# The second MLP's first products begun inside the output products, and low weight parts made by an adding DMA

## The chip, the cores and the metric

The kernel runs on one core of one Trainium2 chip. Its time is the device time of one execution in microseconds (us); of several executions the median counts. The core has a matrix engine (TensorE, PE in the profile), a vector engine (VectorE, DVE), a scalar engine (ScalarE, ACT), GpSimd (POOL) and SyncE (SP), which here only issues DMAs. Each runs its own queue in order; between them there are semaphores.

## The reference

Two layers work on 512 latent tokens and 256 context tokens of 1024 features in fp32. Layer 0 mixes tokens with gated linear attention, layer 1 with 2-D neighbourhood attention of 16 heads; each is followed by a gated MLP with a convolution of width 3 over tokens. What the change touches is the end of layer 1:

```python
x_lat = x_lat + g1_l * o_l                     # o_l: heads @ w_out of the attention
h_l = modulate(x_lat, norm2_g[i], sh2_l, s2_l) # rms_norm(x, g) * (1 + scale) + shift

def conv_ffn(h, w_in, conv_w, conv_b, w_out):
    a, val = jnp.split(h @ w_in, 2, axis=-1)   # 1024 -> 2 x 2816
    ap = jnp.pad(a, ((0, 0), (1, 1), (0, 0)))
    a = ap[:, :-2] * conv_w[0] + ap[:, 1:-1] * conv_w[1] + ap[:, 2:] * conv_w[2] + conv_b
    return (jax.nn.silu(a) * val) @ w_out
```

The result is `x_lat + g2_l * conv_ffn(h_l, ...)`, normalized once more. In layer 1 only the latent tokens go through this MLP.

## The kernel before

**Products in three parts.** Every fp32 operand is held as a rounded high part and a low part that is the rest. `mm3` (L287 to L290) issues three products for one: low weight by high data (L288), high weight by low data (L289), high by high (L290), all into one PSUM group. Names ending in `h` are high parts, in `l` low parts: `wh`, `wl` weights; `hh`, `hl` the normalized tokens `H`; `oh`, `ol` the attention's heads; `uh`, `ul` the MLP's inner values.

**Weights.** `wunit` (L269) brings 128 x 1024 fp32 of weights, 512 KB, by a DMA on SP's queue into one of three buffers `st`. ACT writes the rounded copy `wh` (L283), DVE subtracts, `wl` = `st` - `wh` (L284). Both go into a slot of a ring of five slots of 1024 columns, which the weights take in the order of the program; a slot is free when the last product with its old weights is done.

**Output products of the attention.** `out_group(m, d, a, b)` multiplies two units of `w_no` by the heads of two pairs for one block d of 128 features and tokens a to b, six products into a PSUM bank of the pool `ps_mm` (three banks; the other five banks are `ps_aux`). DVE adds the result, gated, to the residual `xl` (L312). The last two pairs (m = 3) are done in two halves of 256 tokens, eight blocks each.

**Norm.** `Norm` follows block by block. `add` squares a block on ACT (L333, L336) and adds it to `nacc` on DVE (L337). `stats` multiplies `nacc` by ones (TensorE, L344), scales (DVE `ms`, L346), takes the power -1/2 (POOL `rs`, L348) and spreads it over the partitions (TensorE, L351). `apply` makes one block of `H`: `hf` on DVE (L371), `hh` on ACT (L372), `hl` on DVE (L373). The first half's `stats` and `apply` calls stand between the output blocks of the second half; the second half's come after the last block.

**The MLP, `ffn1`.** 2816 inner features are 22 tiles of 128, in six groups of three and one of four. A tile takes two units of `w_fi`, for `a` and `val`; each has 8 x 3 products. `a` goes by ACT into a padded row `apad` (L1079), through the convolution on DVE (L808, L811, L812) and silu on ACT (L813), times `val` (`u`, L1103), split into `uh` (L300) and `ul` (L301). Then the group's units of `w_fo` give output products for eight blocks d. The first group's tiles 0 and 1 are done by `in_first`: their four units of weights, then for the first token half all four product groups (tile, unit), then for the second half all four, each group running its eight blocks k before the next starts. The other tiles run over 512 tokens at once.

**Order.** A scheduler orders each engine's instructions, so that program order is kept only as far as its own estimates do; a table for silu is loaded on ACT once ahead of the first silu. Weights are asked for as slots and buffers come free.

## Time and profile before

| | us |
|---|---|
| median of 3 runs | 1702.51 (1701.19 to 1707.1) |
| the profiled execution | 1703.84 |
| its span | 1702.1 |
| TensorE busy | 1643.6 (97%) |
| DVE busy | 1190.5 (70%) |
| ACT busy | 740.5 (44%) |
| POOL busy | 217.4 (13%) |

In the profiled execution the output products in token halves begin at 1303.03 us of the span, the norm's second half is spread at 1328.60, tiles 0 and 1 end and tile 2 begins at 1347.37, and the first group's output products start at 1358.28. A later group of three tiles begins at 1375.08 and its output products at 1407.74.

To read the rows: a timeline row has start, duration, engine, line, operation, what is written and read, the count, and in brackets the idle time ahead of it with the engine and line that ended it. Starts of pipelined matmuls lie closer than their durations.

### The profile page before, as it was taken

The page shows a single profiled execution, that of the slowest core. Times are in us where ns is not written, and L with a number is a line of the kernel's source. Part 1 is how long each engine was busy: PE and PEld are TensorE (multiplying, and loading weights), DVE is VectorE, ACT ScalarE, POOL GpSimd, SP SyncE. Part 2 cuts the span into 40 slices and gives each one's busy share as a digit, 9 for nine tenths or more (in the row PEclk, how much of TensorE's full clock was granted, in tenths as well). Part 3 has the DMA queues.
Part 4 walks back from the last instruction along what each step waited for, and adds up shares of the span by engine and source line. Part 5 has one row for each costly group of instructions (what it writes and reads, how often), then busy time and mean ns, then how long its engine had stood idle before and what let it go on. Part 6 is the DMA issues. An engine that isn't in the chain of part 4 may idle for free.

```text
span 1702.1 us, 27128 instructions
## 1 busy us (share of the span) xinstructions
PE 1643.6 (97%) x10867; PEld 1409.3 (83%) x10867; DVE 1190.5 (70%) x1973; ACT 740.5 (44%) x1331; POOL 217.4 (13%) x321
## 2 busy tenths in 40 slices
PE   6999999999999999999999999999999999999997
PEld 3768777777899999999999778888887888888887
DVE  4797877785998886878767675666667755555555
ACT  3665746563753432433425454334344522222232
POOL 1021212220000000000000043433332000000000
PEclk9999999999999999999999999999999999999999
DMA  6653513113323332424223042334331233232321
GB/s 257 190 176 108 175 61 107 33 51 137 100 87 124 124 112 68 149 84 159 79 84 102 10 132 92 109 117 130 99 114 61 87 100 95 94 95 75 111 87 50
DMA packets 54190, 179.70 MB, mean 106 GB/s; under 512 B 7024, under 2 KB 10864, under 8 KB 54064
## 3 DMA queue, kind: packets, MB, share of 16 engines
q1 hardware_dynamic: 54064, 177.97, 32.4%
q8 instruction: 85, 1.39, 0.3%
q14 instruction: 41, 0.34, 0.1%
HBM read 173.75 MB, written 2.10 MB: 103 GB/s over the span
## 4 chain that ended last, share of the span: by engine, by line
PE 79%; DVE 10%; ACT 5%; issue 2%; DMA 2%; POOL 2%; SPq 0%; POOLq 0%; ACTq 0%; DVEq 0%
PE mm L288 16%; PE mm L290 15%; PE mm L289 15%; PE aux L288 8%; PE aux L289 8%; PE aux L290 8%; PE mm L1252 2%; PE aux L1235 2%; PE aux L1210 2%; DMA st<-in 1%; DVE t L571 1%; PE aux L650 1%; PE aux L615 1%; ACT wh L283 1%; DVE t L570 1%
## 5 line engine op out<-in xcount | busy, mean ns | idle before, releaser
L288 PE MATMUL mm<-hh,wl 128*128 128x512 f32 (+3 forms) x864 | 306.8, 357 | 5.3 <-ACT hh L372 2.5
L289 PE MATMUL mm<-hl,wh 128*128 128x512 f32 (+3 forms) x864 | 301.4, 350 | 0.4 <-DVE hl L301 0.4
L290 PE MATMUL mm<-hh,wh 128*128 128x512 f32 (+3 forms) x864 | 301.5, 350 | 0.0
L289 PE MATMUL mm<-ul,wh 128*128 128x512 f32 (+1 forms) x544 | 188.3, 347 | 0.2 <-DVE ul L301 0.2
L288 PE MATMUL mm<-uh,wl 128*128 128x512 f32 (+1 forms) x544 | 188.4, 348 | 0.0
L290 PE MATMUL mm<-uh,wh 128*128 128x512 f32 (+1 forms) x544 | 188.4, 347 | 0.0
L288 PEld LDWEIGHTS mm<-hh,wl 128*128 128x128 f32 (+1 forms) x864 | 162.6, 189 | 29.7 <-issue 5.1
L283 ACT ACTIVATE wh<-st 128x1024 fp32r<-128x1024 f32 (+1 forms) x127 | 131.8, 1051 | 121.5 <-issue 69.4
L312 DVE SCALAR_TENSOR_TENSOR xl<-mm,mod,xl 128x512 f32<-128x512 f32 (+1 forms) x168 | 116.1, 697 | 96.2 <-PE mm L290 95.8
L289 PEld LDWEIGHTS mm<-hl,wh 128*128 128x128 f32 (+1 forms) x864 | 163.1, 189 | 18.6 <-issue 0.8
L290 PEld LDWEIGHTS mm<-hh,wh 128*128 128x128 f32 (+1 forms) x864 | 162.9, 189 | 18.6 <-issue 0.8
L284 DVE TENSOR_TENSOR wl<-st,wh 128x1024 fp32r<-128x1024 f32 (+1 forms) x126 | 155.1, 1237 | 30.6 <-ACT wh L283 30.1
L288 PE MATMUL aux<-hh,wl 128*128 128x384 f32 (+2 forms) x496 | 173.8, 351 | 0.0
L289 PE MATMUL aux<-hl,wh 128*128 128x384 f32 (+2 forms) x496 | 173.7, 350 | 0.0
L290 PE MATMUL aux<-hh,wh 128*128 128x384 f32 (+2 forms) x496 | 173.4, 350 | 0.0
L263 ACT ACTIVATE wh<-st 128x512 fp32r<-128x512 f32 (+1 forms) x126 | 94.1, 756 | 164.7 <-issue 57.0
L348 POOL TENSOR_TENSOR rs<-ms,mhalf 128x2 f32<-128x2 f32 (+1 forms) x10 | 10.0, 1004 | 931.5 <-DVE ms L346 931.5
L288 PEld LDWEIGHTS mm<-uh,wl 128*128 128x128 f32 x544 | 102.2, 188 | 15.7 <-ACT uh L300 2.0
L289 PEld LDWEIGHTS mm<-ul,wh 128*128 128x128 f32 x544 | 102.4, 188 | 14.8 <-DVE ul L301 0.4
L264 DVE TENSOR_TENSOR wl<-st,wh 128x512 fp32r<-128x512 f32 (+1 forms) x126 | 104.6, 847 | 12.7 <-ACT wh L263 12.1
L290 PEld LDWEIGHTS mm<-uh,wh 128*128 128x128 f32 x544 | 102.3, 188 | 13.2
L288 PEld LDWEIGHTS aux<-hh,wl 128*128 128x128 f32 x496 | 93.5, 189 | 8.8 <-issue 1.4
(324 smaller groups left out, 3254.7 us busy)
## 6 DMA issues: line engine op xcount, KB each, us to landing
st<-in SPq DMA_DIRECT2D x201, 512.0 KB, 3.7
sa<-in SPq DMA_DIRECT2D x98, 512.0 KB, 3.8
sx<-in SPq DMA_DIRECT2D x14, 512.0 KB, 7.0
xl<-in SPq DMA_DIRECT2D x8, 512.0 KB, 5.5
xc<-in SPq DMA_DIRECT2D x4, 512.0 KB, 7.5
out<-y SPq DMA_DIRECT2D x16, 128.0 KB, 1.7
raw<-in SPq DMA_DIRECT2D x16, 96.0 KB, 2.5
t<-q SPq DMA_DIRECT2D x16, 64.0 KB, 2.1
```

Of the source, the lines that this page charges most:

```text
L263: nc.scalar.activation(hi, s_, AF.Copy)
L264: nc.vector.tensor_sub(lo, s_, hi.bitcast(F32))
L283: nc.scalar.activation(hi, st, AF.Copy)
L284: (eng or nc.vector).tensor_sub(lo, st, hi.bitcast(F32))
L288: mm(out, a[1], b[0], start=first, stop=False, **at)
L289: mm(out, a[0], b[1], start=False, stop=False, **at)
L290: mm(out, a[0], b[0], start=False, stop=last, **at)
L312: nc.vector.scalar_tensor_tensor(x_, ps, gate(l, n, d, rng), x_, OP.mult, OP.add)
L570: nc.vector.tensor_mul(eq, eq, st[h]["q"])
L1210: mm(pss[hh][:, off:off + 256], qe[a_][p_, 128 * t:128 * t + 128], ke[b_][p_, ks], start=i == 0, stop=i == 2)
L1235: nc.tensor.transpose(pT[:, i * 128:(i + 1) * 128], S2[:, o:o + 128], ident)
L1252: mm(po[64 * hh:64 * hh + 64, 128 * t:128 * t + 128], V[:, vs[i], 64 * hh:64 * hh + 64], PTs[hh][:, i * 128:(i + 1) * 128], start=i == 0, ...
```

## The change

**Low parts.** `wunit(..., added=True)` makes the low part without DVE: ACT writes the high part, and also writes `st` times -1 into the low slot, in the same rounded type, so that it holds minus the high part; then a DMA on POOL's queue, with add as its accumulating operation, brings the same weights from HBM once more and adds them there; the sum is rounded into the low slot. The weights in HBM are read twice. This is done for all 44 units of `w_fi` and 22 of `w_fo` of layer 1 and for the last two units of `w_no`: 68 more DMAs of 512 KB, 68 fewer subtractions. `st` is freed by ACT.

**Order of the products.** The two last units of `w_no` and the first of the MLP are asked for in the last head pair, the next two among the first half of the output products. `Begun` holds the weights and banks of tiles 0 and 1. Within the second half of the output products, from block 3 on, and around the second norm's statistics, the first token half is multiplied for three groups at once, (tile 0, a), (tile 0, val), (tile 1, a), block by block (`first3`), in two banks of `ps_aux`, two groups sharing a bank. `stats` is cut into `rms` and `spread_rms`. The weights of the fourth group, (tile 1, val), are asked for behind the second norm's power on POOL (`issue_after` lets what is inside it be placed only behind the given instruction); its first-half products come after the spread. The second token half is then done for all four groups at once, block by block, each behind the `apply` that makes its block, in two banks of `ps_mm`. `in_first` only copies `apad` and finishes. The ring's slots of these four units are, in the order of use, those that the second unit of tile 2 and the first three units of `w_fo` take next.

The places where this moves instructions, in each engine's order. First POOL, from the end of the attention to the end of the program, before (`rs` is the power; buffer numbers stand behind names) and after:

```order
L1225 TENSOR_SCALAR S_12787<-S_12787,ri 128x512 x2
L348 TENSOR_TENSOR rs_13017<-ms_13015,mhalf 128x2
L348 TENSOR_TENSOR rs_13137<-ms_13135,mhalf 128x2
L1067 MEMSET apad_13178 128x1 x2
L1067 MEMSET apad_13179 128x1 x2
L348 TENSOR_TENSOR rs_15597<-ms_15595,mhalf 128x2
L348 TENSOR_TENSOR rs_15753<-ms_15751,mhalf 128x2
```

```order
L1261 TENSOR_SCALAR S_12802<-S_12802,ri 128x512 x2
L286 DMA wl<-in 128x1024 x2
L356 TENSOR_TENSOR rs_13034<-ms_13032,mhalf 128x2
L356 TENSOR_TENSOR rs_13210<-ms_13208,mhalf 128x2
L286 DMA wl<-in 128x1024 x2
L1104 MEMSET apad_13396 128x1 x2
L1104 MEMSET apad_13397 128x1 x2
L286 DMA wl<-in 128x1024 x61
L356 TENSOR_TENSOR rs_15661<-ms_15659,mhalf 128x2
L356 TENSOR_TENSOR rs_15817<-ms_15815,mhalf 128x2
```

After, five of the low parts' DMAs stand ahead of the first power, two of them in this piece; the first of the two right behind the second norm's power, `rs_13210`, is the fourth group's.

Next TensorE, around the second norm's spread (the row with `ident`), one piece of before and two of after; products of `hh` and `hl` are the MLP's:

```order
L290 MATMUL mm<-hh,wh 128x256
L344 MATMUL aux<-ones,nacc 128x2 x2
L288 MATMUL mm<-hh,wl 128x256 x2
L289 MATMUL mm<-hl,wh 128x256
L290 MATMUL mm<-hh,wh 128x256
L351 MATMUL aux<-ident,rs_13137 128x128 x2
L288 MATMUL mm<-hh,wl 128x256
L288 MATMUL aux<-hh,wl 128x256
L289 MATMUL aux<-hl,wh 128x256
```

```order
L293 MATMUL aux<-hl,wh 128x256
L294 MATMUL aux<-hh,wh 128x256
L352 MATMUL aux<-ones,nacc 128x2 x2
L364 MATMUL aux<-ident,rs_13210 128x128
L292 MATMUL aux<-hh,wl 128x256 x2
L364 MATMUL aux<-ident,rs_13210 128x128
L293 MATMUL aux<-hl,wh 128x256
L294 MATMUL aux<-hh,wh 128x256
```

```order
L294 MATMUL mm<-hh,wh 128x256
L292 MATMUL mm<-hh,wl 128x256
L293 MATMUL mm<-hl,wh 128x256
L294 MATMUL mm<-hh,wh 128x256
L292 MATMUL mm<-hh,wl 128x256
L292 MATMUL aux<-hh,wl 128x256
L293 MATMUL aux<-hl,wh 128x256
L294 MATMUL aux<-hh,wh 128x256
L292 MATMUL aux<-hh,wl 128x256
```

The first piece is before, the second after at the same place, the third after some 17 rows later. Before, the last first-half products of the two `a` groups stand between ones and spread, and the first-half products of (tile 0, val), the `aux` rows, behind it. After, the spread's first row stands right behind the ones, and blocks 6 and 7 of the three groups behind it. The third piece shows the end of seven second-half products (into `mm`) and the first products of the fourth group (into `aux`), which read the low part that POOL's DMA makes.

Last ACT, at the end of tiles 0 and 1, before and after (`apad` copies close the tiles' `a`, `wl` and `wh` fill slots, `tt` is silu):

```order
L1079 ACTIVATE apad_13178<-mm 128x256
L1079 ACTIVATE apad_13179<-mm 128x256
L1079 ACTIVATE apad_13178<-mm 128x256
L283 ACTIVATE wh<-st 128x1024 x2
L813 ACT_TABLE_LOAD
L813 ACTIVATE tt<-tt 128x512
L1079 ACTIVATE apad_13179<-mm 128x256
L283 ACTIVATE wh<-st 128x1024
L300 ACTIVATE uh<-u 128x512
L283 ACTIVATE wh<-st 128x1024
L813 ACTIVATE tt<-tt 128x512
```

```order
L1130 ACTIVATE apad_13396<-aux 128x256
L1130 ACTIVATE apad_13397<-aux 128x256
L285 ACTIVATE wl<-st 128x1024
L1130 ACTIVATE apad_13396<-mm 128x256
L283 ACTIVATE wh<-st 128x1024
L1130 ACTIVATE apad_13397<-mm 128x256
L283 ACTIVATE wh<-st 128x1024
L826 ACT_TABLE_LOAD
L826 ACTIVATE tt<-tt 128x512
L285 ACTIVATE wl<-st 128x1024
L283 ACTIVATE wh<-st 128x1024
L304 ACTIVATE uh<-u 128x512
```

Before, two high copies stand ahead of the table load and two behind it in this piece, and the low parts are DVE's. After, low copies stand among them, and the first of them ahead of the `apad` copies from `mm`, which the second token half's products release.

The diff, cut to what is spoken of:

```diff
--- before.py
+++ after.py
@@ -266,7 +266,7 @@
             o += b - a
         return out
 
-    def wunit(src, eng=None, scales=None):
+    def wunit(src, eng=None, scales=None, added=False):
 
 
         n = src.shape[-1]
@@ -281,7 +281,11 @@
                 nc.vector.scalar_tensor_tensor(l_, s_, scales[i], h_.bitcast(F32), OP.mult, OP.subtract)
             return hi, lo
         nc.scalar.activation(hi, st, AF.Copy)
-        (eng or nc.vector).tensor_sub(lo, st, hi.bitcast(F32))
+        if added:
+            nc.scalar.activation(lo, st, AF.Copy, scale=-1.0)
+            nc.gpsimd.dma_start(lo, src, accum_op=OP.add)
+        else:
+            (eng or nc.vector).tensor_sub(lo, st, hi.bitcast(F32))
         return hi, lo
 
     def mm3(out, a, b, first, last, **at):
@@ -337,6 +341,10 @@
             nc.vector.tensor_add(self.acc, self.acc, sq)
 
         def stats(self):
+            self.rms()
+            self.spread_rms()
+
+        def rms(self):
 
             c = self.w // 128
             ps = ps_aux()
@@ -345,7 +353,12 @@
             ms = sml.tile([128, 4], F32, name="ms4", tag="ms4", bufs=2)
             nc.vector.tensor_scalar(ms[:, 0:c], ps[:, 0:2 * c:2], 1.0 / D, EPS, OP.mult, OP.add)
             rs = sml.tile([128, 4], F32, name="rs4", tag="rs4", bufs=2)
-            nc.gpsimd.tensor_tensor(rs[:, 0:c], ms[:, 0:c], mhalf.to_broadcast([128, c]), OP.pow)
+            self.power = nc.gpsimd.tensor_tensor(rs[:, 0:c], ms[:, 0:c], mhalf.to_broadcast([128, c]), OP.pow).ins
+            self.rs = rs
+
+        def spread_rms(self):
+
+            c, rs = self.w // 128, self.rs
             pb = ps_aux()
             for i in range(c):
                 mm(pb[:, i * 128:(i + 1) * 128], rs[:, i:i + 1].to_broadcast([128, 128]), ident, start=True, stop=True)
@@ -1058,6 +1071,30 @@
                     for rng in (LAT, CTX):
                         add_gated(ffn_out(ws, ul, d, rng, 0), 0, 1, d, rng)
 
+    HALVES = ((256, 512), (512, 768))
+
+    class Begun:
+
+
+
+        def __init__(self):
+            self.w, self.ps = {}, [None, None]
+
+        def weights(self, j, which):
+            self.w[j, which] = tuple(t_.rearrange("p (k n) -> p k n", k=KD) for t_ in wunit(w_fi[1, j, which], added=True))
+
+        def banks(self, r, new):
+            self.ps[r] = [new() for _ in range(2)]
+
+        def product(self, r, k, combos):
+            a, b = HALVES[r]
+            for j, which in combos:
+                w = self.w[j, which]
+                mm3(self.ps[r][j][:, 256 * which:256 * which + 256], (w[0][:, k, :], w[1][:, k, :]),
+                    (H[0][:, k, a:b], H[1][:, k, a:b]), k == 0 and which == 0, k == KD - 1, skip_group_check=True)
+
+    begun = Begun()
+
     def ffn1(after):
         n_tok = N_LAT
         with tc.tile_pool(name="ffn1", bufs=4) as pool:
@@ -1080,20 +1117,19 @@
                 return a, b, ps
 
             def in_tile(j):
-                w0 = blocks(wunit(w_fi[1, j, 0]))
+                w0 = blocks(wunit(w_fi[1, j, 0], added=True))
                 in_group(j, 0, w0, LAT)
-                w1 = blocks(wunit(w_fi[1, j, 1]))
+                w1 = blocks(wunit(w_fi[1, j, 1], added=True))
                 return finish(j, [in_group(j, 1, w1, LAT)])
 
             def in_first():
 
-                w = [[blocks(wunit(w_fi[1, j, which])) for which in range(2)] for j in range(2)]
-                psv = [[None, None], [None, None]]
-                for r, rng in enumerate(((256, 512), (512, 768))):
-                    for j in range(2):
-                        in_group(j, 0, w[j][0], rng)
-                        psv[j][r] = in_group(j, 1, w[j][1], rng)
-                return [finish(j, psv[j]) for j in range(2)]
+                us = []
+                for j in range(2):
+                    for r, (a, b) in enumerate(HALVES):
+                        nc.scalar.activation(apad[j][:, a - 255:b - 255], begun.ps[r][j][:, 0:b - a], AF.Copy)
+                    us.append(finish(j, [(a, b, begun.ps[r][j][:, 256:512]) for r, (a, b) in enumerate(HALVES)]))
+                return us
 
             def finish(j, psv):
                 tt = pool.tile([128, n_tok], F32, name="tt", tag="t3", bufs=4)
@@ -1108,7 +1144,7 @@
 
             for grp in GROUPS:
                 us = in_first() + [in_tile(2)] if grp[0] == 0 else [in_tile(j) for j in grp]
-                ws = [lambda d, w=wunit(w_fo[1, j]): tuple(t_[:, d * 128:d * 128 + 128] for t_ in w) for j in grp]
+                ws = [lambda d, w=wunit(w_fo[1, j], added=True): tuple(t_[:, d * 128:d * 128 + 128] for t_ in w) for j in grp]
                 if grp is GROUPS[-1]:
                     last_outs(1, ws, us, 256, ((256, 512), (512, 768)), lambda rng: after(pool, rng))
                     continue
@@ -1261,7 +1297,7 @@
                 sp[pr]["oT"] = (oh, ol)
 
         def out_weights(m):
-            sp[m]["wo"] = [wunit(w_no[k]) for k in (2 * m, 2 * m + 1)]
+            sp[m]["wo"] = [wunit(w_no[k], added=m == 3) for k in (2 * m, 2 * m + 1)]
 
         def out_group(m, d, a=0, b=N_LAT):
 
@@ -1310,6 +1346,9 @@
                 out_weights(m)
             if more:
                 load_raw(nx)
+            else:
+                out_weights(3)
+                begun.weights(0, 0)
             scores(pr, 0)
             if pr:
                 values(pr - 1, 3)
@@ -1351,22 +1390,42 @@
             turn(pr, 3)
             if outs_now and more:
                 out_groups(m, 3, 4)
-        out_weights(3)
         out_group(2, 5)
         values(7, 3)
         out_groups(2, 3, 4)
-        todo = []
         nacc = pool.tile([128, D], F32, name="nacc", tag="acc", bufs=1)
-        for a, b in ((0, 256), (256, 512)):
-            norm = Norm(pool, 1, 1, (N_CTX + a, N_CTX + b), acc=nacc[:, a:b])
-            for d in range(KD):
-                out_group(3, d, a, b)
-                if todo:
-                    todo.pop(0)()
-                norm.add(d)
-            todo += norm.steps()
-        for f in todo:
-            f()
+        norms = [Norm(pool, 1, 1, (N_CTX + a, N_CTX + b), acc=nacc[:, a:b]) for a, b in ((0, 256), (256, 512))]
+        first3 = ((0, 0), (0, 1), (1, 0))
+        for d in range(KD):
+            out_group(3, d, 0, 256)
+            norms[0].add(d)
+            if d == 0:
+                begun.weights(0, 1)
+            if d == 2:
+                begun.weights(1, 0)
+        todo = norms[0].steps()
+        for d in range(KD):
+            out_group(3, d, 256, 512)
+            todo.pop(0)()
+            norms[1].add(d)
+            if d == 0:
+                begun.banks(0, ps_aux)
+            if d >= 3:
+                begun.product(0, d - 3, first3)
+        todo.pop(0)()
+        begun.product(0, 5, first3)
+        norms[1].rms()
+        with tc.issue_after(norms[1].power):
+            begun.weights(1, 1)
+        begun.product(0, 6, first3)
+        begun.product(0, 7, first3)
+        norms[1].spread_rms()
+        for k in range(KD):
+            begun.product(0, k, ((1, 1),))
+        begun.banks(1, ps_mm)
+        for k in range(KD):
+            norms[1].apply(k)
+            begun.product(1, k, first3 + ((1, 1),))
 
     class Final(Norm):
         def apply(self, k):
```

## The prediction

> **What bounds the kernel now.** I read the totals first, then the stretch that the change rewrites, then the stage behind it.
>
> ```profile
> span 1702.1 us, 27128 instructions
> PE 1643.6 (97%) x10867; PEld 1409.3 (83%) x10867; DVE 1190.5 (70%) x1973; ACT 740.5 (44%) x1331; POOL 217.4 (13%) x321
> ...
> L284 DVE TENSOR_TENSOR wl<-st,wh 128x1024 fp32r<-128x1024 f32 (+1 forms) x126 | 155.1, 1237 | 30.6 <-ACT wh L283 30.1
> ```
>
> TensorE is busy for 97% of the span, so an edit that neither shortens products nor removes TensorE idle time buys nothing. The subtractions that go are DVE's, 1.24 us each; DVE is busy for 70%. The table by stretch shows where TensorE leaves room (us; a row ends in granted clock, DMA share, GB/s).
>
> ```profile
> core 0: us, PE busy (x) PEld busy (x) DVE busy (x) ACT busy (x) POOL busy (x), PEclk, DMA share, GB/s
> 1303.03:1347.37 44.34, 39.01 (x305) 37.83 (x304) 36.40 (x81) 23.37 (x46) 2.51 (x6) 0.96 0.23 72
> 1315.30:1326.70 11.40, 8.73 (x60) 8.36 (x59) 10.00 (x27) 7.78 (x16) 0.00 (x0) 0.85 0.00 1
> 1375.08:1407.74 32.66, 32.66 (x145) 27.04 (x144) 18.36 (x22) 11.46 (x15) 0.00 (x0) 1.00 0.39 120
> 1407.74:1424.55 16.81, 16.81 (x74) 13.44 (x72) 7.74 (x11) 2.73 (x4) 0.00 (x0) 1.00 0.14 49
> ```
>
> The last two rows are one steady group of the MLP, first the six product units, then the output products: TensorE has no idle time. Freeing DVE there is worth nothing; it can only be lost. The first row is the last output products, norm and first two MLP tiles: 5.3 us idle. The second row is its tight part, with DVE busy 10.0 of 11.4 us and TensorE 8.7 at a clock of 0.85. The longer idles, by TensorE's timeline (start, duration, in brackets the idle ahead and its releaser):
>
> ```profile
> 1318.81 0.38 PE L288 MATMUL mm<-oh,wl 128*128 128x256 f32 x1 [2.02 <-DVE xl L312]
> 1320.41 0.55 PE L288 MATMUL mm<-hh,wl 128*128 128x256 f32 x1 [0.66 <-DVE xl L312]
> 1328.60 0.71 PE L351 MATMUL aux<-ident,rs 128*128 128x128 f32 x4 [1.36 <-POOL rs L348]
> 1347.01 0.28 PE L288 MATMUL aux<-hh,wl 128*128 128x256 f32 x1
> 1347.13 0.28 PE L289 MATMUL aux<-hl,wh 128*128 128x256 f32 x1
> 1347.37 0.40 PE L288 MATMUL mm<-hh,wl 128*128 128x512 f32 x1
> ```
>
> Starts of 256-token products lie 0.12 us apart at full clock (1347.01 to 1347.13). The stretch holds 96 output products and 192 MLP products: 288 × 0.12 = 34.6 us, with some 1.8 us for the two norms' small products 36.4. So 44.3 − 36.4 = 7.9 us, idle and slow clock together, is all that the early products can win, and 0.3% of the time is 5.1 us.
>
> **The change, its gain first.** DVE paces the second half of the output products. One column block takes an `xl` add, an `nacc` add, `hf` and `hl`:
>
> ```profile
> 1302.40 1.23 DVE L284 TENSOR_TENSOR wl<-st,wh 128x1024 fp32r<-128x1024 f32 x1 [1.74 <-ACT wh L283]
> 1304.87 1.22 DVE L284 TENSOR_TENSOR wl<-st,wh 128x1024 fp32r<-128x1024 f32 x1
> 1315.30 0.48 DVE L371 SCALAR_TENSOR_TENSOR hf<-xl,modA,aux 128x256 f32<-128x256 f32 x1 [1.21 <-PE aux L351]
> 1315.69 0.42 DVE L337 TENSOR_TENSOR nacc<-nacc,sq 128x256 f32<-128x256 f32 x1
> 1316.03 0.47 DVE L371 SCALAR_TENSOR_TENSOR hf<-xl,modA,aux 128x256 f32<-128x256 f32 x1
> 1326.69 0.16 DVE L346 TENSOR_SCALAR ms<-aux 128x2 f32<-128x2 f32 x1 [1.19 <-PE aux L344]
> 1326.77 1.22 DVE L284 TENSOR_TENSOR wl<-st,wh 128x1024 fp32r<-128x1024 f32 x1
> 1313.78 0.72 POOL L348 TENSOR_TENSOR rs<-ms,mhalf 128x2 f32<-128x2 f32 x1 [18.55 <-DVE ms L346]
> 1326.93 1.61 POOL L348 TENSOR_TENSOR rs<-ms,mhalf 128x2 f32<-128x2 f32 x1 [12.44 <-DVE ms L346]
> ```
>
> By starts, `hf` to `nacc` is 0.39 us and `nacc` to the next 0.34, so a block is 3 × 0.39 + 0.34 = 1.52 us. Let T be the first `hf` of the second half: 1315.30 before; I take 1315.5 after, as a negated copy of one weight comes ahead of the last `oh` on ACT (+1 us, mostly lost in waits that exist). Seven blocks later, T+10.6, the second norm's sums can go to TensorE. In before, `ms` to the end of `rs` is 1.85 us (1326.69 to 1328.54), with `rs` at 1.61 beside a 1.22 us subtraction; it took 0.72 without one, and the subtraction is gone. With the ones products `rs` ends at T+12.1 to T+12.7; I take 12.4. That is up to 0.9 us saved.
>
> In TensorE's new order the spread stands right behind the ones product, so TensorE waits there for `rs`, about 1.5 us; then come the spread (0.5), the 18 products of blocks 6 and 7 (2.2) and seven second-half products (0.8): it is at the fourth group at T + 12.4 + 3.5 = T+15.9. It then has 24 + 96 − 7 = 113 products, 13.6 us. Without any wait the two tiles end at T+29.5 = 1345.0, that is 2.4 us ahead of 1347.37. The second half of the tokens has its `hl` at 0.8 us a block against 12 × 0.12 = 1.44 us of products a block, so DVE doesn't bind there. The early products fill waits ahead of T+10.6 whose end DVE sets, and one wait for `rs` stays. So 2.4 us, not 7.9, is what the new order can win.
>
> **The DMA that adds.** It is the unknown. Call L the time from its issue to its landing; it takes the place of a 1.2 us subtraction. Before has no such transfer; the nearest rows (KB each, us to landing):
>
> ```profile
> st<-in SPq DMA_DIRECT2D x201, 512.0 KB, 3.7
> ...
> xc<-in SPq DMA_DIRECT2D x4, 512.0 KB, 7.5
> ...
> t<-q SPq DMA_DIRECT2D x16, 64.0 KB, 2.1
> ```
>
> A plain transfer of the same size takes 3.7 us: the lower end. An eighth of the size takes 2.1, so the other 448 KB are 1.6 us and all 512 some 1.8 of moving. An adding transfer must read its destination as well; that once more makes 3.7 + 1.8 = 5.5, and I take 5.4, some of it overlapping. The upper end is 7.5, the slowest row of this size, if queueing or the issue by POOL costs more.
>
> The Trainium skill's "DMA: Bandwidth & Descriptors", "Anatomy of one DMA — SWDGE (gpsimd) path", gives a DMA issued by GpSimd 2.0 us plus its bytes at 436 GB/s. By that estimate 512 KB take 3.2 us, below the 3.7 that this trace shows for SP's queue, and the sum below would be about −2 us; the page's fit says nothing on adding.
>
> Cover: the weights (0,0), (0,1), (1,0) and the two output weights are issued 10 us and more ahead of use, nothing. In a steady group the group's end frees three slots at once:
>
> ```profile
> 1373.88 2.96 ACT L283 ACTIVATE wh<-st 128x1024 fp32r<-128x1024 f32 x3 [13.82 <-PE mm L290]
> ...
> 1385.98 0.39 PE L288 MATMUL mm<-hh,wl 128*128 128x512 f32 x1
> ```
>
> The first of them is copied by 1374.9 and wanted by the third unit at 1385.98, 11 us later, so L to 11 is hidden; ACT goes from 11.46 + 2.73 to some 14.2 + 9 × 1.05 = 23.6 of a group's 49.5 us and has room. Three places have no cover.
>
> (a) *Fourth group.* Its DMA is queued on POOL behind `rs`, so it lands at T+12.4+L, against T+15.9: a stall of L − 3.5, 1.9 us at 5.4. The tiles end at 1345.0 + L − 3.5 = 1346.9, 0.5 ahead of before. Behind the fourth group on TensorE stands all of the second half.
>
> (b) *First output weights.* In before the four slots come free one after another, and the copies follow, as at 1344.98:
>
> ```profile
> 1342.89 1.28 ACT L813 ACT_TABLE_LOAD   x1
> 1344.18 0.63 ACT L813 ACTIVATE tt<-tt 128x512 f32<-128x512 f32 x1
> 1344.72 0.37 ACT L1079 ACTIVATE apad<-mm 128x256 f32<-128x256 f32 x1
> 1344.98 1.05 ACT L283 ACTIVATE wh<-st 128x1024 fp32r<-128x1024 f32 x1
> 1358.28 0.40 PE L288 MATMUL mm<-uh,wl 128*128 128x512 f32 x1
> ```
>
> In after all four groups go block by block, so all four slots come free only with the last block, and ACT's queue becomes the bound: behind the end of the tiles stand, up to the negated copy of the second output weight, five copies of 1.0 us, the table load 1.28, `tt` 0.6, `uh` 0.6 (its row stands at (c)) and three `apad` of 0.3: 8.4 us. TensorE has 1358.28 − 1347.37 = 10.9 us of tile 2 and 0.7 of the first output weight's products to do, so the second is wanted at 11.6 and lands at 8.4 + L: a stall of L − 3.2, 2.2 us at 5.4 (tile 2's own second half lands at L, wanted at 5.4, just in time). If the subtraction were kept, this would be nothing.
>
> (c) *Last group.* Its last output weight is copied late, and wanted once the last `uh` is done:
>
> ```profile
> 1661.27 1.05 ACT L283 ACTIVATE wh<-st 128x1024 fp32r<-128x1024 f32 x1
> ...
> 1666.95 0.63 ACT L300 ACTIVATE uh<-u 128x512 fp32r<-128x512 f32 x1 [1.68 <-DVE u L1103]
> ```
>
> From 1662.3 to 1667.6: a stall of L − 5.3, 0.1 us.
>
> Each stall of 2 us may also be followed by a slow clock, as after 1320.41; by the clock of the second row of the table that cost 0.15 × 11.4 = 1.7 us. A stall of 2 us alone may not bring one, so I count less than half of one, 0.7.
>
> **Sum** at L = 5.4: −0.5 + 2.2 + 0.1 + 0.7 = +2.5 us. The profiled run took 1703.84 us for its span of 1702.1; the median of the runs shown is 1702.51, 1.3 less. 1702.5 + 2.5 = 1705.0. At L = 3.7: −2.2 + 0.5 = −1.7, 1700.8. At L = 7.5, with a whole slow stretch: +1.6 + 4.3 + 2.2 + 1.7 = +9.8, 1712.3.
>
> **Rivals.** (1) *The adding DMA takes more than I give it, 6.3 to 11 us:* (a), (b) and (c) rise together. The point from which it decides is L = 6.3, where the sum passes +5.1. For it: it is issued by an engine that, in this trace, took 1.61 instead of 0.72 us beside one DVE operation. Against: the DMA share is 0.23 to 0.39 here, so nothing crowds it. At L = 7.5, 1712; at 10, (a) +4.1, (b) 6.8, (c) 4.7, clock 1.7: +17.3, 1720.
>
> The Trainium skill's "SBUF — State Buffer", "SBUF: two separate sides", has the rule against this change: GpSimd can't write a DMA's descriptors while DVE holds the port they share. The trace agrees so far as `rs` goes; no run here shows it for a DMA.
>
> (2) *L over 11, the steady groups stall too:* (L − 11) in each of six groups. At 14: 18 on top of some 28: 1748. Only the distance of all rows from 11 speaks against it.
>
> (3) *Faster:* POOL's queue is empty where SP's is full, so L is 3.2 or less, below the row; and DVE, rid of the subtractions at 1302.40 and 1304.87, brings T ahead by both, 2.4 us, instead of my +0.2. Then (a) and (b) are nothing, and −2.4 − 2.6, with `rs` done at T+12.1 another −0.3, is −5.3: 1697.2. Against: T hangs on a chain of ACT squares and DVE adds in lockstep with TensorE, and the copies go to ACT, ahead of `oh`.
>
> (4) *It doesn't do what it says:* the stretch keeps its idle time since DVE's block time rules; the tiles end at 1347.4 whatever L under 5, and only (b) is left: +1 to +3, 1704 to 1706, inside the forecast.
>
> **Numbers.** A measurement here tells about 0.3% from no change. The forecast, L from 3.7 to 6.3, with (4): 0.50, no measurable change, 1698 to 1708, likeliest 1705. Rival (1): 0.34. Rival (2): 0.04. Rival (3): 0.12, just past that bound. So faster 0.12, same 0.50, slower 0.38. Range 1697 to 1717: it takes in L up to 9 and nearly all of (3), and leaves out (2) and the far end of (1).
>
> **What would show it.** In DMA issues: a row `wl<-in` of POOL's queue, 512 KB, with L beside it; 5.4 is the step. TensorE's timeline: an idle of about 2 us ahead of the first `aux<-hh,wl` after the second spread, released by that DMA, and one of about 2 us at the second output weight near 1358; no idles of 2.02 and 0.66 near 1318 to 1320 any more. POOL: second `rs` at about 0.7 us. In a steady group TensorE still fills its stretch. I'm wrong if the row says over 6.3 with stalls hidden, if the two tiles end after 1348 with L under 6, or if stalls show in steady groups.

## The result, and the profile after

| | before | after |
|---|---|---|
| median of six runs, us | 1704.34 (1701.19 to 1707.1) | 1714.39 (1711.29 to 1716.71) |
| profiled execution, us | 1703.84 | 1711.7 |
| its span, us | 1702.1 | 1709.9 |

The ratio after to before is 1.0054, with a 95% interval of 1.004 to 1.0067: slower by about 9 us. The time lies in the range that was given, but the likeliest case was no change, and it was the first rival that came.

The page of the changed kernel has its first lines, the DMA queues (packets, MB, share of 16 engines) and the DMA issues (KB each, median us to landing) as follows; the last line is of the 68 adding DMAs, from issue to landing.

```profile
span 1709.9 us, 27262 instructions
PE 1646.0 (96%) x10867; PEld 1410.5 (82%) x10867; DVE 1115.6 (65%) x1905; ACT 803.7 (47%) x1399; POOL 278.9 (16%) x389
...
q1 hardware_dynamic: 54064, 177.97, 31.6%
q0 software_dynamic: 9792, 35.66, 11.4%
...
st<-in SPq DMA_DIRECT2D x201, 512.0 KB, 4.5
...
wl<-in POOLq DMA_DIRECT2D x68, 512.0 KB, 8.6
...
DMA to landing us min/median/max: 5.3/8.6/11.7
```

DVE has 75 us less work and ACT 63 us more. The adding DMA takes 8.6 us in the median, from 5.3 to 11.7. TensorE's waits, from its timeline, between the first norm's spread and the second group, with the first product of tile 2 (1347.13):

```profile
1321.12 0.39 PE L293 MATMUL aux<-hl,wh 128*128 128x256 f32 x1 [0.35 <-DVE hl L386]
1324.82 0.49 PE L364 MATMUL aux<-ident,rs 128*128 128x128 f32 x2 [1.20 <-POOL rs L356]
1331.95 0.56 PE L292 MATMUL aux<-hh,wl 128*128 128x256 f32 x1 [3.44 <-DMA wl<-in]
1347.13 0.40 PE L292 MATMUL mm<-hh,wl 128*128 128x512 f32 x1
1360.47 0.47 PE L292 MATMUL mm<-uh,wl 128*128 128x512 f32 x1 [1.92 <-ACT tt L826]
1364.31 1.19 PE L292 MATMUL mm<-uh,wl 128*128 128x512 f32 x2 [2.90 <-DMA wl<-in]
```

The old waits of 2.02 and 0.66 us on DVE are gone. In their place stand 3.44 us in front of the fourth group and 1.92 and 2.90 us in front of the first group's output products. (The row puts the 1.92 down to ACT, whose `tt` ended at 1359.69; but the first output weight's DMA was issued at 1352.69 and landed 7.7 us later, at 1360.38, just ahead of the product at 1360.47. So that DMA came last.) The second output weight's was issued at 1355.59 and landed 8.6 us later, the fourth group's at 1324.72 and 7.2 us later. POOL's rows of the two output weights:

```profile
1352.69 0.86 POOL L286 DMA_DIRECT2D wl<-in  x1 [4.47 <-ACT wl L285]
1355.59 0.86 POOL L286 DMA_DIRECT2D wl<-in  x1 [2.04 <-ACT wl L285]
```

The table by stretch shows what follows each wait (the last number but two is the clock):

```profile
1300.99:1347.13 46.14, 39.58 (x306) 38.13 (x305) 26.05 (x67) 21.20 (x43) 4.39 (x9) 0.96 0.41 92
1331.95:1337.00 5.05, 5.05 (x29) 5.05 (x30) 0.52 (x2) 0.74 (x2) 0.19 (x4) 0.66 0.35 69
1364.31:1370.00 5.69, 5.69 (x14) 4.53 (x15) 0.00 (x0) 1.01 (x2) 0.86 (x1) 0.54 1.06 273
1450.00:1550.00 100.00, 100.00 (x438) 81.70 (x437) 33.61 (x48) 46.22 (x55) 16.50 (x19) 1.00 0.78 193
```

Behind the 3.44 us the clock is 0.66 for 5 us, which costs 0.34 × 5.05 = 1.7 us; behind the two waits at the output products it is 0.54, 0.46 × 5.69 = 2.6 us. (These are means over the windows: the clock is 0.51 to 1335.45 and 0.50 to 1369.60, then full.) In the steady groups TensorE is full, though the DMA share there is 0.78, where before had about 0.3.

To compare executions I cut the end of each at two marks in TensorE's timeline: the first 256-token output product (start), and tile 2's first 512-token product (the two tiles are done). The stage ahead of the start varies by some microseconds from one execution to the next, so these lengths leave it out. **Tiles** is start to tiles done, **rest** from there to the last product of the MLP. (In the two runs marked * one product of tile 2 comes early, among the two tiles; there the mark is tile 2's next one, behind the tiles' last.)

| | ratio to before (95%) | tiles, us | rest, us | sum |
|---|---|---|---|---|
| before | | 44.34 | 343.08 | 387.42 |
| after | 1.0054 (1.004 to 1.0067) | 46.14 | 351.55 | 397.69 |
| order only | 0.9984 (0.9974 to 0.9993) | 40.05 | 344.59 | 384.64 |
| DMA only | 0.9990 (0.9981 to 0.9999) | 42.64 | 343.50 | 386.14 |
| fourth group by subtraction | 1.0031 (1.0021 to 1.0041) | 40.86 | 351.49 | 392.35 |
| first group's by subtraction * | 1.0082 (1.0068 to 1.0096) | 47.36 | 353.26 | 400.62 |
| first two groups' by subtraction * | 1.0029 (1.0019 to 1.0039) | 47.67 | 344.93 | 392.60 |
| DMA for the early units alone | 0.9997 (0.9987 to 1.0008) | 40.83 | 344.62 | 385.45 |
| slots apart | 1.0030 (1.002 to 1.0041) | 47.00 | 344.99 | 391.99 |
| plain copy | 1.0006 (0.9994 to 1.0017) | 42.57 | 347.29 | 389.86 |
| fourth by subtraction, slots apart | 0.9985 (0.9975 to 0.9994) | 40.86 | 344.84 | 385.70 |
| fourth's DMA ahead of the power | 1.0014 (1.0005 to 1.0023) | 40.97 | 351.60 | 392.57 |
| order only, slots apart | 0.9966 (0.9954 to 0.9978) | 40.04 | 343.18 | 383.22 |
| DMA ahead of the power, slots apart | 0.9984 (0.9975 to 0.9994) | 40.96 | 344.90 | 385.86 |

After is 10.3 us longer than before, 1.8 in the tiles and 8.5 behind them.

### The profile page after: what moved, and what is told of

It reads as the page before. It is cut to its first block, busy times and chain, and to the rows that moved or that the text cites. A ratio compares the mean times of both kernels' runs of the same rounds, so it can differ in the third digit from the quotient of the medians.

```text
span 1709.9 us, 27262 instructions
## 1 busy us (share of the span) xinstructions
PE 1646.0 (96%) x10867; PEld 1410.5 (82%) x10867; DVE 1115.6 (65%) x1905; ACT 803.7 (47%) x1399; POOL 278.9 (16%) x389
## 3 DMA queue, kind: packets, MB, share of 16 engines
q0 software_dynamic: 9792, 35.66, 11.4%
## 4 chain that ended last, share of the span: by engine, by line
PE 79%; DVE 9%; ACT 5%; DMA 4%; issue 2%; POOL 2%; SPq 0%; POOLq 0%; ACTq 0%; DVEq 0%
PE mm L292 16%; PE mm L293 15%; PE mm L294 15%; PE aux L292 7%; PE aux L293 7%; PE aux L294 7%; PE mm L1288 2%; PE aux L1271 2%; PE aux L1246 2%; DMA st<-in 1%; DMA sa<-in 1%; PE aux L663 1%; DMA wl<-in 1%; PE aux L628 1%; ACT wh L283 1%
## 5 line engine op out<-in xcount | busy, mean ns | idle before, releaser
L285 ACT ACTIVATE wl<-st 128x1024 fp32r<-128x1024 f32 x68 | 71.7, 1054 | 157.1 <-PE mm L292 128.9
L283 ACT ACTIVATE wh<-st 128x1024 fp32r<-128x1024 f32 (+1 forms) x127 | 131.8, 1046 | 15.9 <-DMA st<-in 10.9
L286 POOL DMA_DIRECT2D wl<-in x68 | 59.9, 885 | 294.9 <-ACT wl L285 187.2
```

What stands on the lines that cost most here:

```text
L283: nc.scalar.activation(hi, st, AF.Copy)
L285: nc.scalar.activation(lo, st, AF.Copy, scale=-1.0)
L286: nc.gpsimd.dma_start(lo, src, accum_op=OP.add)
```

## The experiments

Theory A: the loss is two places where the adding DMA comes uncovered, with the slow clock behind each. Theory B: the doubled traffic costs everywhere. Theory C: the new order itself costs, since four slots come free at once. Diffs are against the changed kernel unless said otherwise.

### One half of the change at a time

Order only:

```diff
-  wunit(..., added=True)      # all five calls
+  wunit(..., added=False)
```

> The change's order of products, all low parts by DVE's subtraction again. Theory A (the loss is two places where the adding DMA comes uncovered, in front of the fourth group and of the first group's output weights, 3.4 and 4.8 us in the changed kernel, and a slow clock behind them): both waits are gone or under 1 us, and the order itself wins a little: 0 to 4 us under the kernel before (ratio 0.9975 to 1.000). Theory B (the doubled traffic slows loads and products everywhere): also gone, ratio about 1.000. Theory C (the new order itself costs, since four slots come free at once): 3 to 6 us slower than before, ratio 1.002 to 1.0035, with a wait in front of the first output products.

DMA only, against the kernel before (with the changed `wunit`):

```diff
-  wunit(w_fi[1, j, ...]), wunit(w_fo[1, j]), wunit(w_no[k])
+  wunit(w_fi[1, j, ...], added=True), wunit(w_fo[1, j], added=True), wunit(w_no[k], added=m == 3)
```

> The kernel before, its order of products kept, with the low parts of the same 68 units by the adding DMA. Theory A: the slots come free one after another, so the DMAs of the first output weights are asked for from 1340 on and are covered; the norm starts up to 2.4 us earlier since two subtractions of DVE are gone: 0 to 3 us under the kernel before, ratio 0.998 to 1.000. Theory B: the steady groups and the place in front of the first output products lose as in the changed kernel: 5 to 8 us slower, ratio 1.003 to 1.005. Theory C: not slower.

Measured 0.9984 and 0.9990: each half alone is a little faster than before, and together they are 0.54% slower. TensorE's longest wait from the first norm's spread on is 0.78 us in the first; the second has one of 1.42 us, on DVE's `xl`, and none on a DMA:

```profile
1360.46 0.50 PE L292 MATMUL mm<-uh,wl 128*128 128x512 f32 x1 [0.78 <-DVE u L1139]
```

```profile
1320.42 0.39 PE L292 MATMUL mm<-oh,wl 128*128 128x256 f32 x1 [1.42 <-DVE xl L316]
...
wl<-in POOLq DMA_DIRECT2D x68, 512.0 KB, 8.2
```

The same 68 DMAs, as long (8.2 us), cost nothing in the old order. Theory B falls. So does C in its plain form, since the order without the DMAs wins. What is left is the two together.

### The fourth group's low part by subtraction

```diff
-  wunit(w_fi[1, j, which], added=True)
+  wunit(w_fi[1, j, which], added=(j, which) != (1, 1))
```

> The changed kernel with the fourth group's low part alone by DVE's subtraction. Theory A: the wait of 3.44 us in front of the fourth group goes, the two tiles end about 3 us earlier (1344 instead of 1347), and since the first output weights follow, all of it is kept: 3 us under the changed kernel, ratio to before about 1.0035. Theory B: no gain beyond 1 us, ratio 1.005. Theory C: as B, the gain is lost again in front of the output products.

Measured 1.0031, 0.0023 or 4 us under the changed kernel. The tiles take 40.86 instead of 46.14 us, so one subtraction instead of one DMA won 5.3 us: about the wait of 3.44 and its slow clock of 1.7. The rest is as long as in the changed kernel (351.49 to 351.55), and the wait there stands unchanged:

```profile
1366.98 1.19 PE L292 MATMUL mm<-uh,wl 128*128 128x512 f32 x2 [2.90 <-DMA wl<-in]
```

### The first output weights by subtraction

```diff
-  wunit(w_fi[1, j, 0], added=True), wunit(w_fi[1, j, 1], added=True), wunit(w_fo[1, j], added=True)
+  wunit(w_fi[1, j, 0], added=j > 2), wunit(w_fi[1, j, 1], added=j > 2), wunit(w_fo[1, j], added=j > 2)
```

> The changed kernel with the low parts of tile 2's two units and the first group's three output weights by DVE's subtraction. Theory A: the waits of 1.92 and 2.90 us near 1360 and the slow clock behind them (some 2.5 us) go: 7 us under the changed kernel, ratio to before about 1.001. Theory B: no gain beyond 1 to 2 us, ratio 1.004 to 1.005. Theory C: a wait of 2 us or more stays there, as four slots still come free at once: a gain of 3 us at most, ratio 1.003 or more.

Measured 1.0082, slower than the changed kernel: a miss. Its timeline shows the old waits cut to 1.01 and 0.18 us, and a new one:

```profile
1365.05 0.50 PE L292 MATMUL mm<-uh,wl 128*128 128x512 f32 x1 [1.01 <-DVE u L1139]
1366.90 0.50 PE L293 MATMUL mm<-ul,wh 128*128 128x512 f32 x1 [0.18 <-DVE ul L305]
1375.10 0.80 PE L292 MATMUL aux<-hh,wl 128*128 128x512 f32 x1 [6.55 <-DMA wl<-in]
...
1363.04 1.80 POOL L286 DMA_DIRECT2D wl<-in  x2 [25.21 <-ACT wl L285]
```

The scheduler put products of the next group's first unit (`aux<-hh,wl`, 512 tokens) among the first group's output products. That unit's low part was asked for at about 1364 and landed at 1375, and TensorE's queue waited for it in order. So the cure of one place made another, by the order of the products. The repair takes the second group's units out of the DMA too:

```diff
-  added=j > 2
+  added=j > 5
```

> The changed kernel with subtractions for tiles 2 to 5 and the output weights of the first two groups, so that no adding DMA is asked for near the first output products (with subtractions for the first group alone, the next group's DMA was waited for instead, 6.55 us). Theory A: the waits at the first output products go, the 3.44 us of the fourth group stay: 6 to 8 us under the changed kernel, ratio to before 1.000 to 1.002. Theory C (a place elsewhere takes the wait over again): a wait of over 3 us at the first unit that is added again, ratio 1.004 or more.

Measured 1.0029, 4 us under the changed kernel and less than expected by its ratio. Its parts say why: the rest falls from 351.55 to 344.93, 6.6 us, as expected, but the tiles grow from 46.14 to 47.67. TensorE's idle time in them is the same (6.5 to 6.6 us), in another order: a wait of 1.11 us and, three products later, 2.66 us in front of the fourth group. The clock behind is 0.51 from 1337.72 to 1343.36, which costs 2.8 us instead of 1.7:

```profile
1337.72 0.58 PE L292 MATMUL aux<-hh,wl 128*128 128x256 f32 x1 [2.66 <-DMA wl<-in]
...
1368.09 0.50 PE L292 MATMUL aux<-hh,wl 128*128 128x512 f32 x1 [1.46 <-DVE wl L288]
```

### Adding or copying

```diff
-  nc.gpsimd.dma_start(lo, src, accum_op=OP.add)
+  nc.gpsimd.dma_start(lo, src.bitcast(FR))
```

> The changed kernel with the same DMAs, of the same weights into the same slots from the same queue, but plain copies that don't add (the low parts then hold the weights themselves, so the products are other numbers). If the adding is what makes the DMA long (it reads its destination too): 3.7 to 5 us to land instead of 8.6, a DMA share of about 0.5 instead of 0.77 in the steady groups, waits of 1 us or less in all three places and 6 to 8 us under the changed kernel, ratio to before about 1.000. If POOL's issue or the sharing with the loads of SP's queue is what makes it long: 7 us or more and no gain beyond 2 us.

Measured 1.0006, in the order of the changed kernel on every engine. From its page, the view of the DMA's line, its timeline and its table by stretch:

```profile
q0 software_dynamic: 9792, 35.66, 7.0%
...
wl<-in POOLq DMA_DIRECT2D x68, 512.0 KB, 4.0
DMA to landing us min/median/max: 3.7/4.0/7.4
1332.63 0.39 PE L292 MATMUL aux<-hh,wl 128*128 128x256 f32 x1 [1.37 <-DMA wl<-in]
1360.25 1.19 PE L292 MATMUL mm<-uh,wl 128*128 128x512 f32 x2 [2.20 <-DMA wl<-in]
...
1450.00:1550.00 100.00, 100.00 (x438) 81.66 (x437) 32.61 (x47) 46.45 (x56) 10.02 (x19) 1.00 0.58 190
```

The same bytes from the same queue land in 4.0 us when they are copied and in 8.6 when they are added; they hold the DMA engines for 7.0% of the span against 11.4%, and in the steady groups the share is 0.58 against 0.78. So it is the adding that makes the DMA long, not POOL's issue. The time falls by 0.0048, 8 us, at the upper end of what was expected, but the waits don't all go under 1 us: the first output weight's vanishes, and of 8.3 us of idle at the two places 3.6 are left. The two copies that are waited for took 5.1 and 5.4 us, not 4.0.

What else goes with the length is what is in flight beside it. In the changed kernel an adding DMA with nothing beside it (issued at 1669.71) took 5.6 us at a DMA share of 0.60; the second output weight's, at a share of 1.05, took 8.6, and one issued at 1360.93, at 1.06, took 10.9. The 28 with three or more other transfers in flight, in the mean over their time, took 8.5 to 11.7 us. Copies with nothing beside them took 3.9 to 4.0. No run changed only this, so that the crowd makes the DMA longer is read from these rows and not shown by an edit.

### Slots that come free one after another

The second token half in another order, all low parts by the adding DMA:

```diff
         for k in range(KD):
             norms[1].apply(k)
-            begun.product(1, k, first3 + ((1, 1),))
+            begun.product(1, k, ((0, 0), (0, 1)))
+        for one in ((1, 0), (1, 1)):
+            for k in range(KD):
+                begun.product(1, k, (one,))
```

> The changed kernel, all low parts by the adding DMA, but the second token half is done block by block for tile 0's two groups only; tile 1's two follow one after the other, so that the slots come free 5.8, 2.9 and 0 us before the tiles end and not all at the end. Theory A, with 8.6 us for the DMA: the first two output weights land at about 7 and 11.6 us behind the end of the tiles, wanted at 10.9 and 11.6: the waits of 1.92 and 2.90 us and the slow clock go, 7 us under the changed kernel, ratio to before 1.000 to 1.002, with the fourth group's wait left. If the slots are not the cause: ratio 1.004 or more.

Measured 1.0030, 0.0024 or 4 us under the changed kernel and so outside the 1.000 to 1.002 expected. The rest falls, as expected, to 344.99 us, 6.6 less; one wait of 1.30 us is left there, and the fourth group's is as it was, with a slower clock behind it (0.50 over 5.41 us), so that the tiles are 0.9 us longer:

```profile
1332.99 0.58 PE L292 MATMUL aux<-hh,wl 128*128 128x256 f32 x1 [3.38 <-DMA wl<-in]
...
1363.75 0.47 PE L292 MATMUL mm<-uh,wl 128*128 128x512 f32 x1 [1.30 <-DMA wl<-in]
```

The first output weight's DMA is issued 1.7 us ahead of the end of the tiles and the second's 2.9 behind it, instead of 5.6 and 8.5 behind; the 1.30 us are a wait for the third's. So the second place is made by the slots: four at once, with ACT's queue of copies and a DMA of 8.6 us behind them.

### The fourth group's DMA ahead of the power

```diff
+        begun.weights(1, 1)
         todo.pop(0)()
         begun.product(0, 5, first3)
         norms[1].rms()
-        with tc.issue_after(norms[1].power):
-            begun.weights(1, 1)
```

> The changed kernel with the fourth group's DMA standing ahead of the second norm's power in POOL's queue, not behind it, still adding. In the changed kernel its minus copy was done at 1319.83 and the DMA began at 1324.72, behind the power. If the place in POOL's queue is the cause: it is issued 4 to 5 us earlier and lands ahead of the fourth group's first product; the wait of 3.44 us goes, 3 to 4 us under the changed kernel, ratio to before 1.003 to 1.0035. If only the length of the DMA counts: the wait stays above 2 us, ratio 1.0045 or more.

Measured 1.0014, 0.2% better than expected; by the lengths of the two profiled executions the gain is 5.1 us (397.69 to 392.57), or 0.3%, with the slow clock that I had left out; the rest is within the two intervals. In the changed kernel (first fence, ACT and POOL) the minus copy was done at 1319.83 and the DMA stood behind the power until 1324.72; here (second) it is issued 3.8 us ahead of the power.

```profile
1318.77 1.06 ACT L285 ACTIVATE wl<-st 128x1024 fp32r<-128x1024 f32 x1 [0.42 <-PE mm L292]
...
1323.90 0.86 POOL L356 TENSOR_TENSOR rs<-ms,mhalf 128x2 f32<-128x2 f32 x1 [11.84 <-DVE ms L354]
1324.72 1.79 POOL L286 DMA_DIRECT2D wl<-in  x2
```

```profile
1322.93 0.91 POOL L286 DMA_DIRECT2D wl<-in  x1 [8.06 <-ACT wl L285]
1326.73 0.88 POOL L356 TENSOR_TENSOR rs<-ms,mhalf 128x2 f32<-128x2 f32 x1 [2.89 <-DVE ms L354]
```

The wait in front of the fourth group is gone, and the tiles take 40.97 us. The place in POOL's queue, together with the DMA's length, was the first cause.

### Both places cured

The edits above two by two: the fourth group by subtraction with the slots apart, and the fourth group's DMA ahead of the power with the slots apart.

```diff
-  wunit(w_fi[1, j, which], added=True)                        # the first of the two
+  wunit(w_fi[1, j, which], added=(j, which) != (1, 1))
-            begun.product(1, k, first3 + ((1, 1),))           # both
+            begun.product(1, k, ((0, 0), (0, 1)))
+        for one in ((1, 0), (1, 1)): ...
+        begun.weights(1, 1)                                   # the second
-        with tc.issue_after(norms[1].power): begun.weights(1, 1)
```

> Both places cured at once, all other low parts still by the adding DMA: the fourth group's low part by DVE's subtraction, and the second token half in the order that frees the slots one after another. If the two places carry the loss, the gains add: the fourth group's 4 us and the slots' 4 us under the changed kernel, 0 to 2 us slower than before, ratio 0.999 to 1.001. If something else of the DMAs costs as well (a slow clock, the steady groups): 1.002 or more.

> The whole change with every DMA kept, both places cured by order alone: the fourth group's DMA ahead of the power, and the slots freed one after another. If the loss is made of the two places: 7 to 8 us under the changed kernel, ratio to before 1.000 to 1.001, and no wait on an adding DMA over 1.5 us. If the DMAs' traffic costs by itself: 1.002 or more.

Measured 0.9985 and 0.9984, both better than expected: the gains of 4 and 4 us were taken from the ratios of the runs with one place cured, and by the lengths they are larger. The second has every one of the 68 DMAs, and only the order of one DMA and of 96 products differ from the changed kernel; it is 0.0070 or 12 us faster, and faster than before. Its tiles and the stretch up to the second group:

```profile
1301.68:1342.64 40.96, 37.80 (x305) 36.55 (x304) 28.11 (x71) 26.10 (x49) 6.18 (x11) 1.00 0.53 117
1342.64:1371.83 29.19, 27.89 (x123) 22.50 (x121) 13.38 (x21) 12.90 (x17) 3.76 (x5) 1.00 0.75 198
...
1357.35 0.47 PE L292 MATMUL mm<-uh,wl 128*128 128x512 f32 x1 [1.30 <-DMA wl<-in]
```

The clock is 1.00 in both stretches, behind the wait of 1.30 us too. The lengths add up: −5.2 us for the first place (46.14 to 40.97), −6.6 for the second (351.55 to 344.99), −11.8 for both (397.69 to 385.86). The loss is these two places, with their slow clock.

### Is the DMA worth anything?

The early units alone by DMA, which no product waits for:

```diff
-  wunit(w_fi[1, j, which], added=True), wunit(w_fi[1, j, 0], added=True), ... wunit(w_fo[1, j], added=True)
+  wunit(w_fi[1, j, which], added=(j, which) != (1, 1)), wunit(w_fi[1, j, 0], added=False), ... wunit(w_fo[1, j], added=False)
```

> The changed kernel with the adding DMA kept only for the five units asked for ahead of the norms (two of the output weights, tile 0's two and tile 1's first); all later low parts by DVE's subtraction. Theory A (order and DMA each win on their own, and lose together where the DMA comes uncovered): no wait on an adding DMA at all; the norm starts some 2 us earlier than with subtractions, as DVE is rid of those ahead of it: 1 to 3 us under the run with the order only, ratio to before 0.997 to 0.998. Theory B (the added traffic itself costs): as the order only, 0.9984.

Measured 0.9997, a miss: no better than the order with subtractions alone (0.9984), the intervals overlapping. The tiles take 40.83 us against 40.05. TensorE waits 1.01 us for the power here (the second line is of the five adding DMAs):

```profile
1327.34 0.49 PE L364 MATMUL aux<-ident,rs 128*128 128x128 f32 x2 [1.01 <-POOL rs L356]
...
DMA to landing us min/median/max: 6.2/8.0/8.4
```

while with subtractions the scheduler left products to fill that place. Ridding DVE of the subtractions gave nothing back.

The order alone with the slots apart:

```diff
-  wunit(..., added=True)      # all five calls
+  wunit(..., added=False)
-            begun.product(1, k, first3 + ((1, 1),))
+            begun.product(1, k, ((0, 0), (0, 1)))
+        for one in ((1, 0), (1, 1)): ...
```

> The new order with subtractions only (ratio 0.9984), and the slots coming free one after another. There the wait in front of the first output products is 0.8 us, released by DVE: that wait is all this can win, and six products a block (0.72 us) against 0.8 us of DVE work a block in the second half can lose as much: within 1 us of the order alone, ratio 0.998 to 0.9995.

Measured 0.9966, better than expected, and the fastest of all: 0.34% under before. Its stretch behind the tiles has no idle time:

```profile
1301.94:1341.98 40.04, 38.08 (x305) 36.58 (x304) 34.51 (x77) 20.52 (x42) 2.51 (x6) 1.00 0.22 69
1341.98:1369.66 27.68, 27.68 (x122) 22.43 (x121) 16.86 (x26) 9.87 (x14) 0.00 (x0) 1.00 0.30 93
```

Of its 1.4 us over the order alone (384.64 to 383.22) 0.8 is the wait that is gone; what the other 0.6 is stays open. So the order of products is what is good in this change, and subtractions serve it better than the DMA that was to make room for it.

## Why the prediction was right in part

**What bounds it, and the two places.** The prediction named both places, what stands behind them and in which queue, and the runs show them there. The clocks of the places came out close: with T the second half's first `hf` (1312.86 in after), `rs` ended at T+11.9 (said: 12.4), TensorE came to the fourth group at T+15.7 (said: 15.9). The second output weight's DMA was issued 8.5 us behind the end of the tiles (said: 8.4).

**The step that failed is the size of L**, "I take 5.4", and with it its upper end of 7.5. The estimate, a small transfer's latency and the bytes moved twice, fits an adding DMA with nothing beside it (5.6; the shortest of the 68 is 5.3). It was used for DMAs that have others beside them, against which I had only put that "nothing crowds it": the three that were waited for took 7.2, 7.7 and 8.6 us, the median is 8.6 and the longest 11.7. In the sum:

| term | said | measured |
|---|---|---|
| fourth group's wait | 1.9 | 3.44, with L = 7.2 (1324.72 to 1331.91) |
| first output weight | no term of its own | 1.92, with L = 7.7 |
| second output weight | 2.2 | 2.90, with L = 8.6 |
| last group | 0.1 | 0, with L = 5.6 |
| slow clock | 0.7 | 1.7 + 2.6 |
| order's gain ahead of the waits | −2.4 | −3.4 (44.34 to 40.96, both places cured) |
| sum | +2.5 | +9.2 |

The first output weight's negated copy ended 5.3 us behind the end of the tiles (1352.39), so at L = 5.4 it would have landed at 10.7, against 10.9 when it was wanted. That margin of 0.2 us was no cover: issued 5.6 us behind the end, it took 7.7 and was waited for. The sum counted this place by the second output weight alone, as L − 3.2, which is 5.4 at 8.6; the two waits together are 4.82. So the formula held, and L was what it had wrong.

**Slow clock.** I counted less than half of one such stretch, and both places had one. Idle of 3.44 us, and of 1.92 and 2.90 us with three products between, was each followed by a clock of 0.66 or 0.54 in the mean over 5 us and more; idle of 1.30 us (both places cured) by none. The Trainium skill's "TensorE: Matmul & The Clock Gate", "Part 1: The HAM clock gate", says that the clock falls to half after an idle window of about 3.4 us and needs about as long of work to return. The first wait agrees with it in length. But shorter ones do it too, and not only two close together: in the run with plain copies one wait of 2.20 us, with no other in the 26 us ahead of it, was followed by a clock of 0.50 for 2.95 us, and with the DMA only 1.42 us and, six products later, 0.25 us by 0.50 for 3.25 us. So a stall of 2 us was enough here, where I had held that it "may not bring one".

**The steady groups** were right: L to 11 is hidden there, and with a median of 8.6 and a longest of 11.7 TensorE has no idle time from 1450 to 1550, and none of 0.2 us or more behind the last row of the waits, up to the MLP's last product. Rival (2) didn't come.

**Rival (1)** is what came, and its price of 1712 at L = 7.5 is near the 1714.39 measured. Against it I had put that the DMA share is only 0.23 to 0.39. That was the share of before; the change itself took it to 0.78, and to 1.05 while the second output weight's DMA was in flight. That the price fits is in part luck: at the median of 8.6 the prediction's own terms give +13.1 (2.7, 5.4, 3.3 and 1.7), 1715.6. The +9.2 measured is made up otherwise: nothing was waited for at the last group (3.3 by its formula), the fourth group's wait and the order's gain cancel, where its terms give 2.7, and the slow clock cost 4.3, not 1.7. And before's median came out at 1704.34, 1.8 above the 1702.5 that the forecast starts from. The likeliest value, 1705 and no measurable change, did not come; the range held the time because it took in this rival up to L = 9. **Rival (3)** was wrong in its cause: DVE without those subtractions moved T by under a microsecond from the start of the output products (12.27 to 11.87 us), and the run with the early DMAs alone was no faster than that without.

**The adding.** The Trainium skill's "Collectives: The Full Stack", "Stop ④ — SDMA + CCE: where bytes move and the add happens", says of a collective's sum that it is done as the bytes stream through, read, read, write, "with the add free in between". In this case adding frees the compute engines, but not the DMA engines: 4.0 us become 8.6, and 7.0% of the span 11.4%.

## What to carry to other kernels

A long transfer that replaces a short instruction is paid for only where its result is wanted soon, so look for the two or three places with the least time between a slot's release and its first product, in every queue that the transfer goes through (here ACT's copies, POOL behind a power, the DMA). Two edits that each win can lose together: an order that frees slots all at once costs 1.4 us with subtractions of 1.2 us (384.64 to 383.22) and 6.6 us with DMAs of 8.6 us (351.55 to 344.99). The length of a transfer should be taken with what will be in flight beside it, as the change itself leaves it, and not from one that runs alone. And a cover of 0.2 us, worked out from an estimate, should be counted as a wait.

## What the runs showed of the hardware that was not expected

- An adding DMA of 512 KB takes 5.3 to 11.7 us, 8.6 in the median; the same as a plain copy 3.7 to 7.4, 4.0 in the median. Alone the two take 5.6 and 3.9 us; in a crowd (DMA share 1.05 to 1.06) the adding one takes 8.6 and 10.9. With five of them in all the median is still 8.0 (6.2 to 8.4); each of the five had loads of SP's queue in flight beside it. So the number of adding DMAs alone doesn't set the length.
- In bytes the two are alike (35.66 MB), in DMA time they are 11.4 and 7.0% of the span; what a GB/s figure shows of such a transfer says little of how long it holds the engines.
- A DMA share of 0.78 instead of 0.31 (1450 to 1550) left TensorE full: 438 products in both. The loads `st` took 4.5 us for 3.7, and TensorE waited for none of them there.
